# First loads in order of use, row norms from the transposed inputs, a last output block in three pieces, and attention outputs made with channels on partitions

## The chip, the core and the metric

The kernel runs on one core of a Trainium2 chip. TensorE (PE in the rows, with PEld its weight loads), VectorE (DVE), ScalarE (ACT), GpSimd (POOL) and SyncE (SP, which here only issues DMAs) each run their own instruction list in order; instructions on different engines wait for each other through semaphores. The metric is the device time of one execution in microseconds (us); less is better.

## The reference

One hybrid encoder layer over 256 tokens of width 2048, in float32. `h` is the normalised input, one large projection of it feeds three branches, and their outputs are gated, projected up, merged and projected once more:

```
h = rms_norm(x, norm_g);  proj = h @ w_in          # split into aq ak av az br bk bv bz bwd bad cq cz ga gb gc
aq, ak = rms_norm per head (8 heads x 128)
ya = chunked_band_attention(aq, ak, av, a_rel_bias) * silu(az)      # softmax over a band of keys, learned bias
yb = rwkv7_time_mix(br, bk, bv, bwd, bad, ...) * silu(bz)           # 16 heads x 64, a recurrence over the tokens
m  = rms_norm(mem, mem_norm_g);  mk, mv = split(m @ w_mem_kv)       # 256 memory tokens
yc = memory_cross_attention(rms_norm(cq), rms_norm(mk), mv) * silu(cz)    # 4 heads x 256
merged = sigmoid(ga)*(ya @ w_up_a) + sigmoid(gb)*(yb @ w_up_b) + sigmoid(gc)*(yc @ w_up_c)
out = x + merged @ w_o
```

## The kernel before

All weights come as one stream of 185 chunks of 1 MB (128 partitions x 2048 floats), issued on the SP queue in the order of use (`wload`, L172 for the first chunk in two halves, L175 for the others), into the tile `raw` with two buffers. `wchunk` turns each half of a chunk into two pieces that TensorE can take: ACT casts it to `whi` (L185), DVE subtracts to get the rest, `wlo` (L187); each has four buffers. The activations are split in the same way (`xh`/`xl` for x, `mh`/`ml` for the memory, `yh`/`yl` for a branch's output, all with channels on partitions).

A projection (`proj`) runs 12 matmuls of 512 columns for each half chunk, 4 each of `whi`·`xh` (L204), `whi`·`xl` (L205) and `wlo`·`xh` (L209). Here this is called a tick. `proj_cm` makes the same products with channels on partitions: 24 matmuls of 256 columns a tick (L222, L223, L225). After each tick, pieces of work that is written as generators (`spawn`, `tick`, `finish`) are put between the matmuls: norms, attention heads, the RWKV recurrence. A generator that yields n is left alone for n ticks. From this program a scheduler makes one fixed list for each engine.

The stages are, in order: the memory projection (32 ticks, ending in the product of `diag` and `ones` at L377); cq and cz, and cross-attention C; the RWKV inputs; gates and up-projections of C; attention A in two halves of four heads (`attn`), while RWKV quarters run between the ticks; gates and up-projections of A, then of B; the output projection in four blocks of 512 columns.

What the change touches:

- The head. `load_split` reads the transposed memory `memT` (then `xT`) in four pieces `xraw` of 512 KB, two buffers, and splits them (ACT L275, DVE L276). The sum of squares of each token is taken from a second copy of the same data with tokens on partitions: `row_rstd` loads `mem` and `x` as `tokraw` (8 DMAs of 512 KB, L259), and ACT squares and sums them (L260).
- `norm_T` normalises q and k, and transposes them; two transposes' worth of PSUM per yield.
- Cross-attention heads (`c_head`) and band-attention heads (`a_head`), one generator each: scores, softmax on DVE and ACT without the division, a transpose of the probabilities (L870), a copy to `apT` (L872), and the product with the values (L876 to L878), whose result has tokens on partitions. DVE divides by the denominator and multiplies by silu(z) there (L881), into `y`. Before the up-projection `to_T` transposes `y` in 16 pieces of 128x128 per branch (L325) and splits it (L326, L327).
- The last heads of A are forced to their end before the gate projection of A:

```
    for g in agen:
        finish(g)
    ...
    yt = spawn(to_T(y_a, yh, yl, 0, 8))
    for j in range(4):
        branch(yh, yl, j, False, yt)
```

- The end. After the last block's matmuls DVE adds the residual in two operations of 128x512 (L958), and SP and ACT each issue one DMA of 256 KB (L960).

Of the kernel before, what the change touches and what calls it, by code (L numbers as in the profile page):

```python
# [17 lines left out]
S = 256  # L18
P = 128
# [14 lines left out]
LATE = 3  # L34
NY = (0, 1, 4)
# [4 lines left out]
def weight_plan():  # L40
# [19 lines left out]
    def attn(h):  # L60
        for o in (O_AQ, O_AK, O_AV, O_AZ):
            plan.append(("in", o + h * 512, 16, 512))

# [30 lines left out]
def _build(ctx, nc, tc, A, out, dbg):  # L94
# [71 lines left out]
    def wload():  # L166
# [12 lines left out]
    def wchunk():  # L179
        raw = first.pop() if first else next(wload())  # L180
# [32 lines left out]

    def proj_cm(xh, xl):
# [24 lines left out]
    V.memset(warm, 0.0)  # L239
    SC.activation(warm[:, 0:1], warm[:, 0:1], AF.Square)  # L240
# [13 lines left out]
    def row_rstd(st_pool, src, dst):  # L254
        ss = t(sm, [P, 2, 2], "ss", bufs=2)
# [5 lines left out]
        G.tensor_tensor(out=dst, in0=ss[:, :, 0], in1=ss[:, :, 1], op=ALU.add)  # L261
        rsqrt_small(dst, dst, 2, 1.0 / D, EPS)

    def load_split(st_pool, src, goff, h, l, mid=None):
        for c in range(4):
            if c:
                yield 2
            raw = t(st_pool, [P, 4, S], "xraw", bufs=2)
            for hf in range(2):
                nc.sync.dma_start(raw[:, hf * 2:hf * 2 + 2, :], src[:, c * 4 + hf * 2:c * 4 + hf * 2 + 2, :])  # L270
                if mid is not None and c == 0 and hf == 0:
                    next(mid)
            for k in range(4):
                kt = c * 4 + k
                SC.activation(h[:, kt, :], raw[:, k, :], AF.Copy, scale=vec[:, goff + kt:goff + kt + 1])  # L275
                V.scalar_tensor_tensor(out=l[:, kt, :], in0=raw[:, k, :], scalar=vec[:, goff + kt:goff + kt + 1],  # L276
                                       in1=h[:, kt, :].bitcast(F32), op0=ALU.mult, op1=ALU.subtract)
# [745 lines left out]
```

## Time and profile before

| | |
|---|---|
| median of 3 runs | 1175.42 us (1173.82 to 1178.39) |
| the profiled execution's own time, its span | 1177.95 us, 1175.9 us |
| TensorE busy, granted clock over the span | 1155.9 us (98%), 0.996 |
| VectorE, ScalarE, GpSimd busy | 784.1, 528.3, 164.2 us |
| HBM read and written | 211.14 MB, 3.67 MB |

Times in the rows are us from the start of the span unless marked ns. A line of the timeline can stand for several equal instructions (x4); its duration is then that of all. What stands in brackets is the idle time of the engine just before, and what ended it.

### The profile page before, as it was taken

What the parts mean: (1) busy time and instruction counts of PE and PEld (TensorE: products, weight loads), DVE (VectorE), ACT (ScalarE), POOL (GpSimd) and SP (SyncE); (2) the same over time, 40 slices, a digit from 0 to 9 for tenths busy, and PEclk for the clock granted to TensorE, in tenths of its full rate; (3) what the DMA queues carried; (4) which work ended last, traced back from release to release, by engine and by line L of the source; (5) the groups of instructions that cost most, each with busy time, mean ns of one, the idle gap of its engine ahead of it and who ended that gap; (6) DMA issues with size and microseconds to landing.
All of it is one profiled execution on the core that took longest, in us unless ns stands there. A gap on an engine that the chain in (4) does not pass through costs nothing.

```text
span 1175.9 us, 15987 instructions
## 1 busy us (share of the span) xinstructions
PE 1155.9 (98%) x6186; PEld 938.6 (80%) x6186; DVE 784.1 (67%) x1320; ACT 528.3 (45%) x654; POOL 164.2 (14%) x234
## 2 busy tenths in 40 slices
PE   7999999999999999999999999999999999999998
PEld 6778888889779778878897778777778877888886
DVE  5574555547959656979685878846787855557443
ACT  6764444445633434444543535543443343444331
POOL 0100000033010214010214110203101203300000
PEclk9999999999999999999999999999999999999999
DMA  8856545465554644554643455454455564555662
GB/s 306 315 217 230 184 140 179 152 199 195 181 213 146 230 167 134 185 205 167 209 162 108 143 189 175 161 179 144 143 190 200 175 206 152 204 179 173 221 218 103
DMA packets 37620, 216.87 MB, mean 184 GB/s; under 512 B 5166, under 2 KB 6958, under 8 KB 13994
## 3 DMA queue, kind: packets, MB, share of 16 engines
q1 hardware_dynamic: 30528, 202.70, 49.5%
q0 software_dynamic: 3936, 9.44, 3.0%
q10 hardware_dynamic: 3082, 3.73, 1.0%
q8 instruction: 48, 0.79, 0.3%
q14 instruction: 26, 0.21, 0.1%
HBM read 211.14 MB, written 3.67 MB: 183 GB/s over the span
## 4 chain that ended last, share of the span: by engine, by line
PE 85%; DVE 5%; DMA 5%; ACT 2%; issue 2%; POOL 1%; SPq 0%; DVEq 0%; ACTq 0%; POOLq 0%
PE pp L204 23%; PE pp L209 23%; PE pp L205 23%; DMA raw<-in_wstream_dram 4%; PE pp L222 3%; PE pp L225 3%; PE pp L223 3%; DVE wlo L187 2%; ACT whi L185 1%; PE ps L325 1%; PE ps L600 1%; PE ps L420 1%; PE ps L396 1%; PE ps L724 1%; PE ps L731 1%
## 5 line engine op out<-in xcount | busy, mean ns | idle before, releaser
L187 DVE TENSOR_TENSOR wlo<-raw,whi 128x1024 fp32r<-128x1024 f32 x370 | 455.2, 1242 | 291.6 <-ACT whi L185 290.1
L185 ACT CAST whi<-raw 128x1024 fp32r<-128x1024 f32 x370 | 382.2, 1049 | 567.2 <-PE pp L205 315.5
L204 PE MATMUL pp<-whi,xh 128*128 128x512 f32 x896 | 363.9, 406 | 0.0
L205 PE MATMUL pp<-whi,xl 128*128 128x512 f32 x896 | 355.7, 397 | 0.0
L209 PE MATMUL pp<-wlo,xh 128*128 128x512 f32 x896 | 246.5, 397 | 3.8 <-DVE wlo L187 3.8
L209 PEld LDWEIGHTS pp<-wlo,xh 128*128 128x128 f32 x896 | 168.5, 188 | 45.7 <-DVE wlo L187 5.1
L204 PEld LDWEIGHTS pp<-whi,xh 128*128 128x128 f32 x896 | 168.7, 188 | 40.2 <-ACT whi L185 1.1
L205 PEld LDWEIGHTS pp<-whi,xl 128*128 128x128 f32 x896 | 168.9, 188 | 38.1 <-issue 0.5
L204 PE MATMUL pp<-whi,yh 128*128 128x512 f32 x192 | 77.3, 403 | 0.0
L205 PE MATMUL pp<-whi,yl 128*128 128x512 f32 x192 | 76.1, 396 | 0.0
L222 PE MATMUL pp<-xh,whi 128*128 128x256 f32 x272 | 67.4, 286 | 0.0
L223 PE MATMUL pp<-xl,whi 128*128 128x256 f32 x272 | 65.5, 279 | 0.0
L204 PE MATMUL pp<-whi,mh 128*128 128x512 f32 x128 | 52.5, 412 | 8.1 <-ACT mh L275 6.3
L209 PE MATMUL pp<-wlo,yh 128*128 128x512 f32 x192 | 52.6, 395 | 0.0
L222 PEld LDWEIGHTS pp<-xh,whi 128*128 128x128 f32 x272 | 51.0, 188 | 0.9 <-issue 0.6
L205 PE MATMUL pp<-whi,ml 128*128 128x512 f32 x128 | 51.5, 404 | 0.0
L223 PEld LDWEIGHTS pp<-xl,whi 128*128 128x128 f32 x272 | 51.1, 188 | 0.5 <-issue 0.2
L205 PE MATMUL pp<-whi,gl 128*128 128x512 f32 x128 | 50.9, 398 | 0.0
L204 PE MATMUL pp<-whi,gh 128*128 128x512 f32 x128 | 50.5, 394 | 0.0
L204 PEld LDWEIGHTS pp<-whi,yh 128*128 128x128 f32 x192 | 36.1, 188 | 8.7 <-issue 0.3
L209 PEld LDWEIGHTS pp<-wlo,yh 128*128 128x128 f32 x192 | 36.1, 188 | 8.7
L205 PEld LDWEIGHTS pp<-whi,yl 128*128 128x128 f32 x192 | 36.1, 188 | 8.1
(231 smaller groups left out, 1219.4 us busy)
## 6 DMA issues: line engine op xcount, KB each, us to landing
raw<-in_wstream_dram SPq DMA_DIRECT2D x184, 1024.0 KB, 4.9
xraw<-in_memT_dram SPq DMA_DIRECT2D x8, 256.0 KB, 7.2
tokraw<-in_mem_dram SPq DMA_DIRECT2D x4, 512.0 KB, 7.0
xraw<-in_xT_dram SPq DMA_DIRECT2D x8, 256.0 KB, 6.7
tokraw<-in_x_dram SPq DMA_DIRECT2D x4, 512.0 KB, 5.9
Tu<-scrt POOLq DMA_DIRECT2D x4, 512.0 KB, 5.5
xr<-in_x_dram POOLq DMA_DIRECT2D x8, 256.0 KB, 4.1
out_dram<-xr POOLq DMA_DIRECT2D x6, 256.0 KB, 3.3
```

Source lines behind the costliest of these rows:

```text
L185: SC.copy(hi, sl)
L187: V.tensor_tensor(out=lo, in0=sl, in1=hi.bitcast(F32), op=ALU.subtract)
L204: T.matmul(acc[tt], xh[:, kt + k2, sl], hv[:, k2], start=(kt + k2 == 0), stop=False)
L205: T.matmul(acc[tt], xl[:, kt + k2, sl], hv[:, k2], start=False, stop=False)
L209: T.matmul(acc[tt], xh[:, kt + k2, sl], lv[:, k2], start=False, stop=(last and k2 == 1))
L222: T.matmul(acc, hv[:, k2], xh[:, kt + k2, :], start=(kt + k2 == 0), stop=False)
L223: T.matmul(acc, hv[:, k2], xl[:, kt + k2, :], start=False, stop=False)
L225: T.matmul(acc, lv[:, k2], xh[:, kt + k2, :], start=False, stop=(kt + k2 == 15))
L325: T.transpose(bank[:, kk, tt * P:tt * P + P], src[:, tt, (k + kk) * P:(k + kk + 1) * P], ident)
L396: T.matmul(sc[:, tt, :], cqT[:, hh * 2 + k, tt * P:tt * P + P], mkT[:, hd * 2 + k, :], start=(k == 0), stop=(k == 1))
L420: T.matmul(pv[:, tt, :], pT[:, k, tt, :], mv[:, k, hd * 256:(hd + 1) * 256], start=(k == 0), stop=(k == 1))
L600: T.matmul(scs[par][:, c].rearrange("p a u -> p (a u)"), BK[rs, b, c].rearrange("p a u -> p (a u)"), AX[rs, b, c, par:par + 2, :].rearrang ...
```

## The change

- Head: the first chunk comes in three pieces (512, 512 and 1024 columns) and the first piece of `memT` in three, in turn; `vec` goes to the ACT queue; 16 small matmuls on a constant tile run on TensorE before the first weight lands (`WARMUP`). `mem` is no longer read and `x` only for the residual: each `xraw` piece is squared in place by ACT once it is split, DVE adds the four rows of it into `part` (`sq_part`), and TensorE sums over partitions with `ones` (`row_rstd`).
- cz and az are made by `silu_T` with channels on partitions, by `proj_cm` in 128-column blocks instead of `proj` in one of 512.
- Heads go in pairs (`c_heads`, `a_heads`). DVE scales the probabilities by 1/denominator before the transpose. The operands of the product with the values are swapped, so its result has channels on partitions: `split_y` multiplies by silu(z) and writes the split pair `yth`, `ytl` directly. `to_T` is gone for C and A.
- The gate projection of A's first block comes first, and then the heads are brought to their end (`branch`).
- `norm_T` and `to_T` issue eight transposes together instead of four.
- The last output block is made in three accumulators (`proj_last`): token tile 0, then token tile 1 in two halves of 256 columns, with the last two ticks' operands held, so that each part ends, is added and stored for itself.

```
+            for a, b in ((0, 512), (512, 1024), (1024, 2048)):
+                nc.sync.dma_start(raw[:, a:b], A["wstream"][i][:, a:b])
...
+    def sq_part(st_pool, raw, part, c):
+        SC.activation(raw, raw, AF.Square)
+        V.tensor_tensor(out=raw[:, 0:2, :], in0=raw[:, 0:2, :], in1=raw[:, 2:4, :], op=ALU.add)
...
+            V.tensor_tensor(out=raw[:, 0, :], in0=raw[:, 0, :], in1=raw[:, 1, :], op=ALU.add)
+            V.tensor_tensor(out=part, in0=part, in1=raw[:, 0, :], op=ALU.add)
+    def row_rstd(tot, dst):
+        bank = psum([P, 2])
         for tt in range(2):
-            for hf in range(2):
-                xt = t(st_pool, [P, 1024], "tokraw", bufs=2)
-                nc.sync.dma_start(xt, src[tt * P:(tt + 1) * P, hf * 1024:(hf + 1) * 1024])
-                SC.activation(xt, xt, AF.Square, accum_out=ss[:, tt, hf:hf + 1])
+            T.matmul(bank[:, tt:tt + 1], tot[:, tt * P:tt * P + P], ones[:, 0:1], start=True, stop=True)
+        V.tensor_copy(dst, bank)
...
+    def silu_T(pl, xh, xl, dst):
+        for i in range(4):
+            acc = proj_cm(xh, xl)
+            zr = t(pl, [P, 512], "qn", bufs=2)[:, :S]
+            V.tensor_tensor(out=zr, in0=acc, in1=rstd_bc, op=ALU.mult)
+            SC.activation(dst[:, i, :], zr, AF.Sigmoid)
+            V.tensor_tensor(out=dst[:, i, :], in0=zr, in1=dst[:, i, :], op=ALU.mult)
+    def split_y(pl, pv, z, yh, yl):
+        y = t(pl, [P, 512], "qn", bufs=2).rearrange("p (a b) -> p a b", b=S)
+        V.tensor_tensor(out=y, in0=pv, in1=z, op=ALU.mult)
+        SC.copy(yh, y)
+        V.tensor_tensor(out=yl, in0=y, in1=yh.bitcast(F32), op=ALU.subtract)
...
+    wld = wload()
+    raw0 = next(wld)
+    xr0 = t(mp, [P, 4, S], "xraw", bufs=2)
+    nc.scalar.dma_start(vec, A["vec"])
+    nc.sync.dma_start(xr0[:, 0:1, :], A["memT"][:, 0:1, :])
+    next(wld)
+    nc.sync.dma_start(xr0[:, 1:2, :], A["memT"][:, 1:2, :])
+    nc.sync.dma_start(xr0[:, 2:4, :], A["memT"][:, 2:4, :])
+    next(wld)
...
+    for i in range(WARMUP):
+        T.matmul(wps[:64, :64], warm, warm, start=True, stop=True)
...
-            finish(yt)
+        for g in yt or ():
+            finish(g)
...
+    def a_heads(half, h0, qT, kT, av, zT):
+        bias = a_bias(half * 4 + h0)
+        yield 1 + h0
+        scs = [psum([P, 384]) for _ in range(2)]
...
+        for i in range(2):
+            bt, sc = bias[:, i, :], scs[i]
+            pr = t(ap_, [P, 384], "apr", bufs=2)
...
+            V.reciprocal(den, den)
+            V.tensor_scalar(out=pr[:, 0:128], in0=pr[:, 0:128], scalar1=den[:, 0:1], scalar2=None, op0=ALU.mult)
+            V.tensor_scalar(out=pr[:, 128:384], in0=pr[:, 128:384], scalar1=den[:, 1:2], scalar2=None, op0=ALU.mult)
+            prs.append(pr)
+        yield 4
+        pts = [psum([P, 3, P]) for _ in range(2)]
+        pTs = []
+        for i in range(2):
+            for b in range(3):
+                T.transpose(pts[i][:, b, :], prs[i][:, b * P:(b + 1) * P], ident)
...
+        yield 2
+        pv = psum([P, 2, S])
+        for i in range(2):
+            hc = slice((h0 + i) * P, (h0 + i) * P + P)
+            T.matmul(pv[:, i, :], av[:, 0, hc], pTs[i][:, 0:2].rearrange("p a b -> p (a b)"), start=True, stop=False)
+            T.matmul(pv[:, i, P:S], av[:, 1, hc], pTs[i][:, 2], start=False, stop=True)
+        ks = slice(half * 4 + h0, half * 4 + h0 + 2)
+        split_y(ap_, pv, zT[:, h0:h0 + 2, :], yah[:, ks, :], yal[:, ks, :])
...
+        if j == 3:
+            for acc, tt, c0, n in proj_last(gh, gl, 16, 2):
+                V.tensor_tensor(out=xr[:, tt, c0:c0 + n], in0=acc, in1=xr[:, tt, c0:c0 + n], op=ALU.add)
+                eng = nc.scalar if c0 else nc.sync
+                eng.dma_start(out[tt * P:(tt + 1) * P, j * 512 + c0:j * 512 + c0 + n], xr[:, tt, c0:c0 + n])
```

The order of ACT at the program's start, before. `raw` is the weight chunk, `xraw` a piece of `memT`, `mh` its rounded split; the numbers tell buffers of one name apart.

```order
L185 CAST whi_122<-raw_105 128x1024
L275 ACTIVATE mh_103<-xraw_108,vec_72 128x256 x2
L185 CAST whi_126<-raw_105 128x1024
L275 ACTIVATE mh_103<-xraw_108,vec_72 128x256 x2
L275 ACTIVATE mh_103<-xraw_154,vec_72 128x256 x4
L351 DMA cst_73<-in_cst_dram 128x384
L352 DMA eye_3_74<-in_eye_dram 128x256
L185 CAST whi_167<-raw_165 128x1024
L185 CAST whi_171<-raw_165 128x1024
```

The same place on ACT now.

```order
L442 CAST whi_138<-raw_105 128x512
L308 ACTIVATE mh_103<-xraw_107,vec_72 128x256
L442 CAST whi_138<-raw_105 128x512
L308 ACTIVATE mh_103<-xraw_107,vec_72 128x256 x3
L291 ACTIVATE xraw_107<-xraw_107 128x1024
L451 CAST whi_140<-raw_105 128x1024
L308 ACTIVATE mh_103<-xraw_183,vec_72 128x256 x4
L428 DMA cst_73<-in_cst_dram 128x384
L429 DMA eye_3_74<-in_eye_dram 128x256
L291 ACTIVATE xraw_183<-xraw_183 128x1024
L191 CAST whi_200<-raw_198 128x1024
L191 CAST whi_204<-raw_198 128x1024
```

A square of 128x1024 (L291) now stands ahead of the cast of the first chunk's second half, and another ahead of the cast of the second chunk (`raw_198`).

DVE in the second half of attention A, before: `apr` are the probabilities of one head, `Xu` and `tmu` belong to the RWKV loop. The rows begin where the loop ends.

```order
L638 TENSOR_TENSOR Xu_6091<-Xu_6091,tmu_6139 128x8
L688 COPY BK_6615<-vL_1551 64x128
L642 COPY tmx_6375<-Xu_6091 128x256
L688 COPY BK_6615<-vL_1551 64x128 x7
L688 COPY Tu_6614<-vL_1551 64x128 x8
L187 TENSOR_TENSOR wlo_6549<-raw_6541,whi_6547 128x1024
L854 SCALAR_TENSOR_TENSOR apr_6419<-ps_6416,bias_6344 128x128
L856 SCALAR_TENSOR_TENSOR apr_6419<-ps_6416,bias_6344 128x256
L859 TENSOR_REDUCE nmx_6422<-apr_6419 128x1
L860 TENSOR_REDUCE nmx_6422<-apr_6419 128x1
```

The same place on DVE now.

```order
L743 TENSOR_TENSOR Xu_6470<-Xu_6470,tmu_6559 128x8
L793 COPY Tu_7034<-vL_1824 64x128
L747 COPY tmx_6852<-Xu_6470 128x256
L793 COPY Tu_7034<-vL_1824 64x128
L793 COPY BK_7035<-vL_1824 64x128 x2
L193 TENSOR_TENSOR wlo_6970<-raw_6966,whi_6968 128x1024
L956 SCALAR_TENSOR_TENSOR apr_6778<-ps_6772,bias_6654 128x128
L958 SCALAR_TENSOR_TENSOR apr_6778<-ps_6772,bias_6654 128x256
L961 TENSOR_REDUCE nmx_6781<-apr_6778 128x1
L962 TENSOR_REDUCE nmx_6781<-apr_6778 128x1
```

Softmax of heads 2 and 3 stands at the same place on DVE as before, behind the whole loop.

TensorE there, before: `pp` are projection accumulators (those of zb), `apT` transposed probabilities, `avv` the values, and the last row transposes the probabilities of head 2.

```order
L209 MATMUL pp_6222<-wlo_6450,xh_89 128x512 x2
L876 MATMUL ps_6480<-avv_6023,apT_6402 128x128
L877 MATMUL ps_6480<-avv_6023,apT_6402 128x128
L878 MATMUL ps_6480<-avv_6023,apT_6402 128x128
L204 MATMUL pp_6221<-whi_6452,xh_89 128x512
...
L209 MATMUL pp_6222<-wlo_6454,xh_89 128x512 x2
L870 MATMUL ps_6502<-cst_73,apr_6419 128x128 x3
```

TensorE there now.

```order
L215 MATMUL pp_6659<-wlo_6897,xh_88 128x512 x2
L985 MATMUL ps_6927<-apT_6877,avv_6361 128x256
L986 MATMUL ps_6927<-apT_6877,avv_6361 128x128
L985 MATMUL ps_6927<-apT_6879,avv_6361 128x256
L986 MATMUL ps_6927<-apT_6879,avv_6361 128x128
L976 MATMUL ps_6936<-cst_73,apr_6778 128x128 x3
L976 MATMUL ps_6937<-cst_73,apr_6791 128x128 x3
L210 MATMUL pp_6658<-whi_6899,xh_88 128x512
```

The transposes of heads 2 and 3 now stand together, one tick earlier than that of head 2 stood: ahead of the last tick of zb's projection instead of behind it.

## Rows read from the trace of the kernel before

**Rows 1.** The page, busy time of each engine and share of the span.

```profile
PE 1155.9 (98%) x6186; PEld 938.6 (80%) x6186; DVE 784.1 (67%) x1320; ACT 528.3 (45%) x654; POOL 164.2 (14%) x234
```

**Rows 2.** What TensorE waited for: us in total, times, longest.

```profile
PE pp L209 <- DVE wlo L187: 4.3, 4, 2.5
PE ps L876 <- ACT apT L872: 2.2, 1, 2.2
PE pp L204 <- ACT whi L185: 1.8, 2, 1.5
PE ps L870 <- ACT apr L863: 0.5, 1, 0.5
```

**Rows 3.** Timeline of the head: start, duration, engine, line, operation, tiles, count [idle].

```profile
4.52 1.04 ACT L185 CAST whi<-raw 128x1024 fp32r<-128x1024 f32 x1 [2.30 <-DMA raw<-in_wstream_dram]
6.34 1.22 PE L204 MATMUL pp<-whi,mh 128*128 128x512 f32 x2 [6.34 <-ACT mh L275]
8.48 1.04 ACT L185 CAST whi<-raw 128x1024 fp32r<-128x1024 f32 x1 [1.80 <-DMA raw<-in_wstream_dram]
9.66 1.71 ACT L275 ACTIVATE mh<-xraw,vec 128x256 fp32r<-128x256 f32 x4
10.70 2.46 DVE L276 SCALAR_TENSOR_TENSOR ml<-xraw,vec,mh 128x256 fp32r<-128x256 f32 x6
13.47 2.00 ACT L185 CAST whi<-raw 128x1024 fp32r<-128x1024 f32 x2 [1.30 <-DMA raw<-in_wstream_dram]
14.93 0.40 PE L204 MATMUL pp<-whi,mh 128*128 128x512 f32 x1
...
39.80 0.50 PE L204 MATMUL pp<-whi,mh 128*128 128x512 f32 x1 [1.54 <-ACT whi L185]
72.06 1.20 PE L209 MATMUL pp<-wlo,mh 128*128 128x512 f32 x4 [0.50 <-DVE wlo L187]
104.02 0.59 PE L377 MATMUL ps<-diag,ones 128*128 128x256 f32 x2
```

**Rows 4.** TensorE with 128-column transposes (L325), and with `proj_cm` (L225).

```profile
1047.13 0.60 PE L325 MATMUL ps<-cst,merged 128*128 128x128 f32 x4
...
1047.80 0.39 PE L205 MATMUL pp<-whi,yl 128*128 128x512 f32 x1
...
207.20 1.10 PE L225 MATMUL pp<-xh,wlo 128*128 128x256 f32 x8
```

**Rows 5.** Timeline of the second half of attention A.

```profile
708.22 0.19 DVE L636 TENSOR_TENSOR tmu<-Tu,Xu 128x31 f32<-128x31 f32 x1 [2.64 <-DMA Tu<-scrt]
744.08 1.10 PE L209 MATMUL pp<-wlo,xh 128*128 128x512 f32 x4
744.12 1.77 DVE L688 COPY Tu<-vL 64x128 f32<-64x128 f32 x8
745.01 0.39 PE L876 MATMUL ps<-avv,apT 128*128 128x128 f32 x2
745.93 1.23 DVE L187 TENSOR_TENSOR wlo<-raw,whi 128x1024 fp32r<-128x1024 f32 x1
747.07 0.28 DVE L854 SCALAR_TENSOR_TENSOR apr<-ps,bias 128x128 f32<-128x128 f32 x1
747.60 0.28 DVE L859 TENSOR_REDUCE nmx<-apr 128x1 f32<-128x128 f32 x1
749.64 0.17 DVE L866 RECIPROCAL rden<-den 128x2 f32<-128x2 f32 x1
```

**Rows 6.** Windows: us, busy PE, PEld, DVE, ACT, POOL, granted clock, DMA share, GB/s.

```profile
676.00:680.00 4.00, 1.55 (x4) 1.13 (x4) 3.77 (x5) 1.99 (x2) 0.17 (x1) 0.78 0.00 0
756.00:760.00 4.00, 4.00 (x21) 3.72 (x21) 2.35 (x5) 0.74 (x2) 0.00 (x0) 0.59 0.49 201
```

**Rows 7.** Timeline of the end.

```profile
1170.78 1.29 DVE L958 TENSOR_TENSOR xr<-pp,xr 128x512 f32<-128x512 f32 x2 [9.36 <-PE pp L209]
1172.10 0.36 ACTq L960 DMA_DIRECT2D out_dram<-xr  x1
```

More of the change, by code (lines that the diff above doesn't have):

```diff
@@ L60, in attn @@
     def attn(h):
-        for o in (O_AQ, O_AK, O_AV, O_AZ):
+        for o in (O_AQ, O_AK, O_AV):
             plan.append(("in", o + h * 512, 16, 512))
+        for i in range(4):
+            plan.append(("in", O_AZ + h * 512 + i * 128, 16, 128))
     rk(0)
@@ L212, in proj, with proj_last, run @@
         return acc
+    def proj_last(xh, xl, nk, split):
+        accA = pp.tile([P, 512], F32, name=nm("pp"), tag="pp", bufs=4)
+        accB = [pp.tile([P, 512], F32, name=nm("pp"), tag="pp", bufs=4) for _ in range(2)]
+        parts = [(accA, 0, 0, 512)] + [(accB[i][:, :256], 1, i * 256, 256) for i in range(2)]
+        kt = 0
+        def run(part, kt, hv, lv):
+            acc, tt, c0, n = part
+            sl = slice(tt * P, tt * P + P)
+            cs = slice(c0, c0 + n)
+            for k2 in range(2):
+                T.matmul(acc, xh[:, kt + k2, sl], hv[:, k2, cs], start=(kt + k2 == 0), stop=False)
+                T.matmul(acc, xl[:, kt + k2, sl], hv[:, k2, cs], start=False, stop=False)
+            for k2 in range(2):
+                T.matmul(acc, xh[:, kt + k2, sl], lv[:, k2, cs], start=False, stop=(kt + k2 == nk - 1))
+        held = []
+        while kt < nk:
+            for hi, lo in wchunk():
+                held.append((kt, hi.rearrange("p (k n) -> p k n", n=512), lo.rearrange("p (k n) -> p k n", n=512)))
+                kt += 2
+                if kt <= nk - 2 * split:
+                    for part in parts:
+                        run(part, *held[-1])
+                    held.clear()
+                tick()
+        for part in parts:
+            for h in held:
+                run(part, *h)
+            yield part
     def proj_cm(xh, xl):
@@ L270, in load_split @@
                 nc.sync.dma_start(raw[:, hf * 2:hf * 2 + 2, :], src[:, c * 4 + hf * 2:c * 4 + hf * 2 + 2, :])
-                if mid is not None and c == 0 and hf == 0:
-                    next(mid)
             for k in range(4):
[L274 to L277, printed above, removed]
+                split_kt(raw[:, k, :], goff, c * 4 + k, h, l)
+            sq_part(st_pool, raw, part, c)
     def norm_T(pl, acc, rstd, nh, hd, gcols, dst):
@@ L468, in _build @@
         finish(g)
-    dump("y_c", y_c)
     c_st.close()
@@ L884, in _build @@
     agen = []
     def attn(half):
-        cols = slice(half * 512, half * 512 + 512)
         acc = proj(xh, xl, 16)
@@ L898, in attn @@
         evac_scale(acc, rstd_x, av)
-        acc = proj(xh, xl, 16)
-        evac_silu(acc, y_a[:, :, cols])
+        zT = t(ap_, [P, 4, S], "azT")
+        silu_T(ap_, xh, xl, zT)
         finish(kn)
-        bias = [a_bias(half * 4)]
-        for h in range(4):
-            agen.append(spawn(a_head(half, h, qT, kT, av, bias), 2 * h))
+        for h0 in (0, 2):
+            agen.append(spawn(a_heads(half, h0, qT, kT, av, zT)))
     rk_proj(2)
@@ L911, in _build @@
     evac_silu(proj(xh, xl, 16), zb0)
-    for g in agen:
-        finish(g)
+    for j in range(4):
+        branch(yah, yal, j, False, agen if j == 0 else None)
     at_st.close()
-    dump("y_a", y_a)
-    g_st = ExitStack()
-    gp = pool(g_st, "ga")
-    yh = t(gp, [P, 8, S], "yh", F32R)
-    yl = t(gp, [P, 8, S], "yl", F32R)
-    yt = spawn(to_T(y_a, yh, yl, 0, 8))
-    for j in range(4):
-        branch(yh, yl, j, False, yt)
-    g_st.close()
     dump("merged_a", merged)
```

268 lines of the change are left out of this document (142 added, 126 removed).

## The prediction

> **What bounds the kernel now.** I read the busy times first, then TensorE's list of waits, then the timeline around each wait, and the granted clock of the windows behind them. TensorE is busy for 98% of the span, DVE for 67% [rows 1]. So only what TensorE executes, what it waits for, and the two ends of the program count; work taken from or given to DVE or ACT costs something only where TensorE then waits for it. TensorE has four places of loss [rows 2, 3]: the start, where its first matmul comes at 6.34; the memory stage (1.54 at 39.80, 0.50 at 72.06, the rest of the 1.8 on `whi` in the same stage); 3.8 of the 4.3 on `wlo`, which fall between 656 and 681 in an RWKV quarter; and the last heads of attention A, 2.2 on `apT` and 0.5 on `apr`. After two of these the clock drops to its lower level, 1.2 GHz, for a time: the window from 676 shows 0.78 and that from 756 shows 0.59 [rows 6]. The matmuls of one tick take 12 x 0.233 = 2.80 us: the four that begin at 744.08 give way at 745.01 [rows 5].
>
> The sum is made against the profiled execution's own 1177.95 us (span 1175.9 and 2.05 around it). That is 2.5 above the median of the runs; I carry the difference over to the median.
>
> **The head.** The start is earlier, but the start is not what decides. The second half of the first chunk is there at 8.48 and the second chunk at 13.47: each cast ends a wait for its DMA [rows 3]. The bytes ahead of the second chunk in the queues are the same as before, since the eight `tokraw` loads stand behind it. So the landing stays near 13.4, and what can be won early is lost again in the wait for it. Now a square stands ahead of each of these casts on ACT, and it works in place: it has to wait until DVE has read the piece for `ml`. By hand: the last two `mh` of the first piece end at about 7.9, their `ml` at 8.3; the square (I price it as the cast of the same 1024 columns, 1.04) ends at 9.3, the cast of the third part of chunk 0 at 10.35; four `mh` take 1.71 [rows 3] and end at 12.05. On DVE that half's `wlo` (1.14, from 745.93 to 747.07 [rows 5]) ends at 11.5 and four `ml` at 0.41 (six took 2.46 [rows 3]) at 13.1; the second square ends at 14.1 and the first cast of chunk 1 at 15.2. The third tick, which began at 14.93, begins at about 15.2: later, in spite of a first matmul at about 5.0.
>
> From there I find no wait of TensorE: chunk 2 is issued near 11.6, no longer kept behind `tokraw` loads, and each later cast by hand is done 2 to 5 us before its tick. The 30 ticks left take 84.0 and the 16 transposes of the two key norms 1.75, which puts the product at L377 at 101.0 instead of 104.02 [rows 3]: a gain of 3.0. What goes is the late issue of chunks 2 and 4, the 1.54 and the 0.50. Ends: if the second chunk were no limit, 5.0 + 32 x 2.80 + 1.75 = 96.4, a gain of 7.6; if the new way to the norm (DVE copy, GpSimd, ACT) holds ACT for another 1.5, as the old one did before 39.80, and the third tick comes 1 later, a gain of 0.5. I take 2.8, near the hand schedule.
>
> The 16 small matmuls ahead of the first weight bear on the clock. Before, the four matmuls of the first two rows of TensorE in the head stood 0.43 to 0.61 apart, half the rate of later ones (the two from 6.34 take 1.22 [rows 3]). The Trainium skill, TensorE: Matmul & The Clock Gate, "What's actually happening", holds that the throttled state is the default and that activity releases it. By that the second tick would run at 2.4 GHz and end at 13.2; with the clock as the head showed it before, it would end at 15.5. The third tick's cast at 15.2 lies between, so the gain is 3.0 by the one and 2.7 by the other.
>
> **Transposes.** 32 transposes of `y` for C and A go. Four cost 0.67 - 0.23 = 0.44, from 1047.13 to the second matmul behind them at 1047.80 [rows 4]; 32 are 3.5 us of TensorE time in a stage where it never idles. Gain 3.5. Their casts and subtractions move into `split_y`, one 512-wide operation each, beside other matmuls.
>
> **silu by `proj_cm`.** 384 matmuls of 512 columns become 768 of 256. Eight of 256 take 1.10 [rows 4] and four of 512 take 1.10 [rows 5]; the rows differ by less than their last digit, which over 96 such groups is at most 1.0. I take 0.5 lost, the ends 0 and 1.0. The last block's smaller matmuls add 0.1 in the same way, the 4 matmuls with `ones` as much again at most.
>
> **End.** Before, DVE added the first of the last two accumulators from 1170.78, when it was done, and both until 1172.07; the last DMA was issued at 1172.10, 3.8 before the end [rows 7]. The last accumulator now ends where the second one did, two matmuls behind the first, at about 1171.25 for DVE, and only 256 columns are added then, some 0.4 (half of 0.65, and a start): 1171.65, 0.4 earlier. The DMA is half as large; if all its time went with size that would be 1.9, if none, nothing; I take 0.2, near the lower end. Gain 0.6, ends 0.4 and 2.3.
>
> **Last heads of A.** The wait of 2.2 + 0.5 and the slow window behind it (4 x 0.41 = 1.6) go, 4.3 in all, because the heads are no longer forced through behind each other. But I see a new wait on the same softmax. DVE works without a break from 708.22, where the RWKV loop starts, to 745.93 [rows 5], and softmax of head 2 stands behind that loop in both orders. Between these points the new order lacks 12 copies of 64x128 (8 take 1.77, so 2.65), two 512-wide products (1.3), two of 128 (0.6) and one `wlo` (1.14), and has four scalings (a 128 and a 256 wide one 0.53, from 747.07 to 747.60 [rows 5]: 1.06) and seven operations of 256 (0.33 each, 2.3) more. Head 2's softmax begins 2.3 earlier, at 744.7. The chain to its reciprocal took 2.57 (747.07 to 749.64 [rows 5]); one `wlo`, a copy and the scaling lie in it now, so the probabilities are ready at 749.0, and those of head 3, behind five more copies, at 750.9. TensorE, however, wants them one tick earlier than before: the tick that ended at 745.01, then both heads' value products (0.65 more than the one head's there), 0.2 for `proj_cm`: 745.9. It waits 3.1 for head 2 and 1.6 for head 3, 4.7, and behind that loses some 1.3 to the lower clock (between the 0.9 and 1.6 of [rows 6]). 6.0 against 4.3: 1.7 lost. Ends: 4.3 gained if DVE comes to head 2 five us sooner, 4 lost if it comes two later.
>
> **Hidden edits.** DVE gets 0.7 x 8 and 0.33 x 14 more for the sums of squares, and the products, scalings and splits of the pairs; with 33% of DVE idle [rows 1] I cost them at nothing outside the place above. Uncovered, a pair's softmax takes 6.2 from its first operation to the second head's end (744.7 to 750.9; 2.3 of it are one `wlo` and RWKV's copies), while C's pairs leave two ticks, 5.6, and A's four. C may wait 0 to 1.5, the first half of A as much; I take nothing. The 3.8 on `wlo` from 656 on stay: the same DVE burst stands there. Grouped transposes of the norms change nothing in sum.
>
> Sum: -2.8 - 3.5 + 0.5 + 0.2 - 0.6 + 1.7 = -4.5. 1177.95 becomes 1173.45, the median 1170.9.
>
> **Rivals.**
> - Heads 2 and 3 do not wait. The loop on DVE starts with a DMA [rows 5]; if that lands some 5 us sooner against TensorE's ticks, the 4.3 go and nothing comes: the sum is then -4.5 - 1.7 - 4.3 = -10.5, the median 1164.9. Against it: the rows of DVE ahead of the loop are as good as the same.
> - The head reaches its floor of 96.4: 7.6 for 2.8, median 1166.1. For it: 4 MB less are read in the first 60 us. Against it: the second chunk's landing, and ACT's squares ahead of the casts.
> - The head gives nothing (0.5 for 2.8): median 1173.2. For it: ACT works in order, and each square can hold a cast back.
> - Slower: pairs wait on DVE wherever they stand. The place is the pair's transposes, at C twice and in A four times; the price is the pair's 6.2 plus the `wlo` that the order puts between, less the ticks left. It decides from the point where DVE starts a pair more than half a tick late at C (5.6 left) or 5 late at A. Then C costs 2 x 3 with the lower clock, the first half of A 6.0, the second 2 more: +14, median 1184.9. For it: the second half, where I count on it already. Against it: C and A's first half have no RWKV loop of that length on DVE.
>
> **Numbers.** The forecast case 0.45 (its own range 1167.5 to 1174), no wait of heads 2 and 3 0.20, head at its floor 0.10, head without gain 0.13, slower 0.12. The bound between a change and none is 0.5%, 5.9 us: faster is below 1169.5, slower above 1181.3. Faster: both early cases and a third of the forecast's, 0.45; slower 0.11, nearly all of its case; the rest, 0.44, within. The range goes from 1162, where part of the first two rivals together lies, to 1179, part of the slow case.
>
> **What would show it.** First matmul near 5 but the third tick at 15 to 15.5; squares on ACT ahead of the casts at about 8.3 and 13.1; L377's successor at 101; no wait of TensorE between 16 and 100; no `to_T` of `y_c`, `y_a`; waits of about 3 and 1.6 on the transposes of `apr` in the second half of A, with a lower clock behind, and none in the first; 3.8 on `wlo` in the RWKV quarter before. It is wrong if the memory stage ends before 98 or after 103, if the last heads wait under 2 or over 8, or if C waits over 2.

## The result, and the profile after

The changed kernel takes 1162.82 us (median of 4 runs, 1162.67 to 1164.07), the kernel before 1176.62 beside it: 0.9887 of the time, with an interval of 0.9864 to 0.991. That is 13.8 us less against a forecast of 4.5. The profiled execution is of 1162.67 us, its span 1160.9, the granted clock 0.998.

The page of the changed kernel, busy time of each engine, share and instructions (it answers to [rows 1]):

```profile
PE 1141.2 (98%) x6610; PEld 961.0 (83%) x6610; DVE 804.7 (69%) x1378; ACT 528.9 (46%) x655; POOL 167.5 (14%) x232
```

TensorE is busy for 14.7 us less, and yet it executes 424 instructions more. The 32 transposes that went are worth 3.5 of it; no other step of the forecast takes work from it. So something made each matmul shorter. The list of what TensorE waited for in the changed kernel (us in total, times, longest; one row of 0.2 is left out; it answers to [rows 2]) shows at the same time that waits took no part in the gain; they add up to 16.1, against 15.3 before (of which 6.3 ahead of the first matmul):

```profile
PE pp L215 <- DVE wlo L193: 3.9, 3, 2.8
PE pp L210 <- ACT whi L191: 3.5, 2, 2.0
PE ps L423 <- ACT warm L420: 2.7, 1, 2.7
PE ps L976 <- ACT BKt L758: 2.1, 1, 2.1
PE ps L976 <- DVE apr L968: 1.3, 1, 1.3
PE pp L210 <- ACT mh L308: 0.9, 1, 0.9
PE pp L210 <- ACT whi L451: 0.9, 1, 0.9
PE ps L705 <- DVE AX L717: 0.6, 1, 0.6
```

Where the time went is seen in TensorE's timeline, at the group of four 512-column matmuls that [rows 5] show from 744.08 to 745.01. First such a group on `xh` in the changed kernel, with the instruction behind it, then one on `yth`, then eight of 256 columns in `proj_cm`:

```profile
742.41 1.07 PE L215 MATMUL pp<-wlo,xh 128*128 128x512 f32 x4
743.31 0.59 PE L985 MATMUL ps<-apT,avv 128*128 128x256 f32 x2
...
889.68 1.10 PE L215 MATMUL pp<-wlo,yth 128*128 128x512 f32 x4
890.62 0.40 PE L210 MATMUL pp<-whi,yth 128*128 128x512 f32 x1
...
260.49 1.12 PE L262 MATMUL pp<-xh,wlo 128*128 128x256 f32 x8
261.45 0.28 PE L259 MATMUL pp<-xh,whi 128*128 128x256 f32 x1
```

In the kernel before, the instruction behind the eight of [rows 4]:

```profile
208.14 0.81 PE L396 MATMUL ps<-mkT,cqT 128*128 128x256 f32 x3
```

Four on `xh` now give way after 0.90 us (before: 0.93), four on `yth` after 0.94, and eight of 256 columns after 0.96 (before 0.94, from 207.20 to 208.14). Averaged over all matmuls that directly follow another of the same size without a wait, from start to start, 512 columns take 227.6 ns (before 233.3), 512 columns on `yth` and `ytl` 233.3, 256 columns 119.9 (before 117.6). The clock is at its upper level in both (granted 0.996 before and 0.998 now over the span). Nothing in these instructions was changed; what differs is where their operands lie in a partition of the on-chip memory. In the built programs the weights `whi`, `wlo` start at 160 modulo 256 both times. `xh`, `xl`, `mh`, `yh`, `gh` start at 224 before and at 160 after, because small tiles that the change no longer needs lay in front of them (the pool of small tiles shrank from 832 to 512 bytes, and a reserved area from 16384 to 4096). `yth` starts at 224.

### The profile page after: what moved, and what is told of

The parts are those of the page before. It is cut to its first block, busy times and chain, and to the rows that moved or that the text cites. A ratio compares the mean times of both kernels' runs of the same rounds, so it can differ in the third digit from the quotient of the medians.

```text
span 1160.9 us, 16874 instructions
## 1 busy us (share of the span) xinstructions
PE 1141.2 (98%) x6610; PEld 961.0 (83%) x6610; DVE 804.7 (69%) x1378; ACT 528.9 (46%) x655; POOL 167.5 (14%) x232
## 4 chain that ended last, share of the span: by engine, by line
PE 82%; DVE 9%; DMA 4%; issue 2%; ACT 1%; POOL 1%; SPq 0%; ACTq 0%; POOLq 0%; DVEq 0%
PE pp L210 21%; PE pp L211 20%; PE pp L215 20%; PE pp L259 4%; PE pp L260 4%; PE pp L262 4%; DVE wlo L193 3%; DMA raw<-in_wstream_dram 3%; DVE Xu L743 1%; DVE tmu L741 1%; DMA Tu<-scrt 1%; PE pp L232 1%; PE pp L234 1%; PE pp L231 1%; ACT whi L191 1%
## 5 line engine op out<-in xcount | busy, mean ns | idle before, releaser
L210 PE MATMUL pp<-whi,xh 128*128 128x512 f32 x768 | 309.2, 403 | 1.5 <-ACT whi L191 1.5
L211 PE MATMUL pp<-whi,xl 128*128 128x512 f32 x768 | 300.8, 392 | 0.0
L259 PE MATMUL pp<-xh,whi 128*128 128x256 f32 x528 | 131.3, 287 | 0.0
L260 PE MATMUL pp<-xl,whi 128*128 128x256 f32 x528 | 129.6, 284 | 0.0
L259 PEld LDWEIGHTS pp<-xh,whi 128*128 128x128 f32 x528 | 101.2, 192 | 1.1 <-issue 0.6
L260 PEld LDWEIGHTS pp<-xl,whi 128*128 128x128 f32 x528 | 101.4, 192 | 0.6 <-issue 0.2
L262 PE MATMUL pp<-xh,wlo 128*128 128x256 f32 x528 | 74.1, 283 | 0.0
L262 PEld LDWEIGHTS pp<-xh,wlo 128*128 128x128 f32 x528 | 68.1, 192 | 0.0
L210 PE MATMUL pp<-whi,yth 128*128 128x512 f32 x128 | 51.9, 405 | 0.0
L211 PE MATMUL pp<-whi,ytl 128*128 128x512 f32 x128 | 50.5, 395 | 0.0
```

Of the source, the lines that this page charges most:

```text
L210: T.matmul(acc[tt], xh[:, kt + k2, sl], hv[:, k2], start=(kt + k2 == 0), stop=False)
L211: T.matmul(acc[tt], xl[:, kt + k2, sl], hv[:, k2], start=False, stop=False)
L259: T.matmul(acc, hv[:, k2], xh[:, kt + k2, :], start=(kt + k2 == 0), stop=False)
L260: T.matmul(acc, hv[:, k2], xl[:, kt + k2, :], start=False, stop=False)
L262: T.matmul(acc, lv[:, k2], xh[:, kt + k2, :], start=False, stop=(kt + k2 == 15))
```

## The experiments

The theory after this was that the distance of the two start addresses modulo 256 sets the spacing. The experiments move tiles without changing a matmul. In the first pair the edit is one line ahead of `mhalf`, the same in both kernels:

```
+    G.memset(t(sm, [P, 16], "pad"), 0.0)      # 64 unused bytes
```

**e1: before, 64 bytes more.** 

> The kernel before with one unused tile of 64 bytes per partition in the pool of small tiles, so that every tile behind it (xh, xl, mh, ml, yh, yl, gh, gl) starts 64 bytes further; the list of instructions is otherwise the same. Theory A (the start address of the operand that TensorE loads as weights sets the spacing of the matmuls: xh stood at 96 modulo 128 bytes before and stands at 32 in the changed kernel): the 512-column matmuls go from 233.3 ns apart to about 227, the 256-column ones of proj_cm from 117.7 to 119.9; 4032 x 6.4 ns less and 816 x 2.1 ns more, -24 us, about 1152 to 1157 (some of it may come back as waits). If the period is 256 bytes and not 128, no change or an unknown one. Theory B (the spacing follows from the work beside the matmuls, which the change altered): 233.3 ns and 1176 us as before.

Measured: 1175.55 us, ratio 0.9995 (0.9981 to 1.0009). `xh` stands at 32, 128 from the weights; 512 columns take 232.7 ns, 256 columns 119.3. No change: a distance of 128 is not as good as 0.

**e2: after, 64 bytes more.** 

> The changed kernel with the same unused tile of 64 bytes: xh, mh, yh, gh start at 96 modulo 128 again. Theory A: the matmuls on them go back to 233.3 ns (512 columns) and 117.7 (256 columns): about 3300 x 6.3 ns more and 1680 x 2.1 ns less, +15 to +17 us, 1178 us, a little slower than the kernel before; the rest of the change is then worth nothing or less. Theory B: 227 ns and 1163 us as they are.

Measured: 1173.37 us, ratio 0.9969 (0.9956 to 0.9982). `xh` is back at 224, the distance of before, and so are the spacings: 233.3 and 117.5 ns. TensorE's timeline of e2, the same four matmuls and their successor:

```profile
746.33 1.09 PE L215 MATMUL pp<-wlo,xh 128*128 128x512 f32 x4
747.26 0.59 PE L986 MATMUL ps<-apT,avv 128*128 128x256 f32 x2
```

0.93 again. So 64 unused bytes take back some 10 us (10.6 between the two medians, 9.6 by their ratios to the kernel before). At equal addresses the change itself is worth 3.5 against the kernel before beside it (1176.9; by the interval 2.1 to 5.2), and 4.3 between the two profiled executions (spans 1175.9 and 1171.6), of which that of before (1177.95) was above its median.

**e3: before, the reserved area cut to 4096 bytes.**

```
-    nc = bacc.Bacc("TRN2", target_bir_lowering=False, num_devices=1)
+    nc = bacc.Bacc("TRN2", target_bir_lowering=False, num_devices=1, dynamic_dma_scratch_size=4096)
```

> The kernel before with the reserved area at the start of the on-chip memory at 4 KB instead of 16 KB, as the changed kernel has it; all tiles shift by 12288 bytes, a multiple of 256. Theory A: no change, 233.3 ns and 1176 us. Rival C (the smaller reserved area is what made the matmuls faster, through GpSimd's DMAs or the absolute addresses): 227 ns and 1155 to 1163 us.

Measured: 1176.33 us, ratio 0.999 (0.9979 to 1.0001), spacings 233.3 and 117.7. It shifts `xh` and the weights by 12288, a multiple of 256, and does nothing.

**e4: a kernel of matmuls alone.** It leaves the layer out and copies x to the output. Eight stationary and eight moving tiles start 32 bytes apart modulo 256 (`sa` 128, `sb` 160, ... `sh` 96; `ma` to `mh` the same), and each pair runs 24 times, with 512 columns (L40, stationary `s`) and with 256 (L45, stationary `m`). 

> Not the layer: x is copied to the output, and beside it TensorE runs 64 groups of 24 matmuls of 512 columns (weights from tile sa to sh, moving columns from tile ma to mh) and then 64 groups of 24 of 256 columns with the two roles exchanged. The tiles' starts step by 32 bytes: sa and ma at 128 modulo 256, sb and mb at 160, and so on to sh and mh at 96. No other engine works. Theory A: within the 512-column groups the spacing depends on the weight tile alone, 227 ns for starts of 32 modulo 128 and 233 for 96, the same for all m at a given s, and in the second half of the grid 117.7 to 120 by tile. Theory B: all 512-column groups have one spacing.

Groups of e4 by line and tile (moving, then stationary tile; count; busy us, mean ns of one). The mean is longer than the spacing, since a matmul overlaps the next one:

```profile
L40 PE MATMUL pa<-mb,sb 128*128 128x512 f32 x24 | 5.6, 391 | 0.0
L40 PE MATMUL pa<-mb,sh 128*128 128x512 f32 x24 | 5.7, 392 | 0.0
L40 PE MATMUL pa<-mb,sd 128*128 128x512 f32 x24 | 5.8, 396 | 0.0
...
L45 PE MATMUL pa<-sb,mb 128*128 128x256 f32 x24 | 3.0, 283 | 0.0
L45 PE MATMUL pa<-sh,mb 128*128 128x256 f32 x24 | 2.9, 277 | 0.0
L45 PE MATMUL pa<-sd,mb 128*128 128x256 f32 x24 | 3.0, 279 | 0.0
```

With 512 columns the pairs at distance 0 (here `mb`, `sb`) are the shortest, 227 to 228 ns from start to start (only `ma`, `sa`, which comes first, has longer matmuls at its beginning); the eight whose stationary tile lies 64 below the moving one (`sh`) follow with 229; the other 48 take 232 to 234, `sd`, the distance of before, among them. The expectation's theory A, in which the stationary tile alone decides, is out: with `sb` the spacing is 228 or 233 by the moving tile. With 256 columns distance 0 is slow (119.3 to 119.7), and a moving tile 64 below the stationary one is fast, but only for five of the eight such pairs (113.7 to 114.7; the other three 117.7 to 117.8). That part isn't settled by the distance alone.

**e5: before, 192 bytes more**, the line of e1 with 48 floats, so that `xh` starts at 160.

```
+    G.memset(t(sm, [P, 48], "pad"), 0.0)      # 192 unused bytes
```

> The kernel before with an unused tile of 192 bytes in the pool of small tiles: xh, mh, yh, gh then start at 160 modulo 256, as whi and wlo do. Theory A2 (what counts is the distance modulo 256 between the start of the weight operand and that of the moving operand; the grid gives 226.7 ns for 0, 229.3 for -64 and 233 to 234 for the others): 512-column matmuls from 233.3 to 226.7, 256-column ones from 117.7 to 119.9; 4032 x 6.6 less and 816 x 2.2 more, -25 us, 1151 to 1157 after some new waits. That is more than the whole change gave. Theory B2 (64 bytes more slowed the changed kernel for another reason): 233 ns and 1176 us.

Measured: 1159.82 us, ratio 0.9857 (0.9841 to 0.9873), span 1158.9; 512 columns take 227.7 ns, 256 columns 119.9. TensorE's timeline of e5:

```profile
733.72 1.08 PE L209 MATMUL pp<-wlo,xh 128*128 128x512 f32 x4
734.63 0.38 PE L877 MATMUL ps<-avv,apT 128*128 128x128 f32 x2
```

192 unused bytes in the old kernel give as much as the whole change (by the medians 3 us more, but the two intervals overlap). The expectation was 25 us; the gain is 16. The shorter matmuls are there: 4032 x 5.6 ns less and 816 x 2.3 ns more make 20.7 us less, not 25, since 512 columns came to 227.7 and not to the 226.7 of the grid. More waits came with them: 6.3 on `wlo` (before 4.3) and 2.3 on `whi` (1.8 [rows 2]), 2.5 more in sum. What took the last 2 us stays open.

**e10: after, 192 bytes more.** `xh` at 96, 64 below the weights; the edit is e5's line.

> The changed kernel with 192 bytes more in the pool of small tiles: xh, mh, yh, gh at 96 modulo 256, 64 below whi and wlo. By the grid 512-column matmuls take 229.3 instead of 226.7 there (some 3200 x 2.5 = 8 us more) and 256-column ones 114 to 117 instead of 119.9 (1680 x 3 to 6 = 5 to 10 us less): 1161 to 1166 us, with both spacings as named. If the period or the sign were wrong, 233 ns or 119.9 would show.

Measured: 1164.59 us, ratio 0.9905 (0.9885 to 0.9924). Spacings 229.5, 233.3 on `yth`, and 114.0 with 256 columns. TensorE's timeline of e10, twice eight of 256 columns on the same tiles:

```profile
201.08 1.11 PE L262 MATMUL pp<-xh,wlo 128*128 128x256 f32 x8
202.02 3.62 PE L494 MATMUL ps<-mkT,cqT 128*128 128x256 f32 x16
...
261.08 1.07 PE L262 MATMUL pp<-xh,wlo 128*128 128x256 f32 x8
261.99 0.28 PE L259 MATMUL pp<-xh,whi 128*128 128x256 f32 x1
```

0.91 at 261.08 against 0.96 in the changed kernel. All three spacings came as the grid had them. But the 114.0 is a mean of two levels: those from 201.08 give way after 0.94, on the same tiles at the same distance modulo 512 and with the clock at its upper level (granted 1.00 from 200 to 204 and from 260 to 264). At this distance the 256-column matmuls run at some 113 or some 118 ns for several ticks and then change; so the distance alone doesn't decide it.

**e6: after, every pair aligned.** `yth` moves to 160, and `proj_cm` writes its weights 64 bytes further on, for its moving operand to lie 64 below them.

```
-    def wchunk():
+    def wchunk(o=0):
...
-            hi = t(wp, [P, 1024], "whi", F32R, bufs=4)
+            hi = t(wp, [P, 1088], "whi", F32R, bufs=4)[:, o:o + 1024]
...
-        for hi, lo in wchunk():
+        for hi, lo in wchunk(16):
...
+    G.memset(t(ycp, [P, 16], "padr"), 0.0)
...
```

The tiles of `wlo` are cut in the same way, and the reserved area goes from 4096 to 2048 bytes to make room.

> The changed kernel with starts chosen from the grid: yth and ytl at 160 modulo 256 (an unused tile of 64 bytes beside them), and for proj_cm the weight pieces written 64 bytes further into tiles that are 256 bytes longer (the reserved area goes from 4096 to 2048 bytes to make room). Theory A2: the up-projections of C and A go from 233.3 to 226.7 ns (384 x 6.6 = 2.5 us) and the 256-column matmuls from 119.9 to 114 (1680 x 5.9 = 9.9 us): 1150.5 us, 1149 to 1156. Rival (with ACT, DVE and DMAs beside it the gain of the grid does not come for 256 columns): 119 to 120 ns, 1160 us.

Measured: 1159.52 us, ratio 0.9857 (0.9834 to 0.9881). Spacings 227.6, 227.3 on `yth`, and 117.2 with 256 columns instead of 114. It is e10's pair of levels again, with the slow one in most groups: eight from 129.81 give way after 0.94, eight from 458.29 after 0.91. New waits took part of the rest, 4.7 on `whi` (3.5 in the changed kernel) and 2.1 on `AX` (0.6).

**e11: e6 at e10's place**, moving operands at 96 and `proj_cm`'s weights at 160; beside e6's edit:

```
+    G.memset(t(cp, [P, 48], "padc"), 0.0)
...
-    G.memset(t(ycp, [P, 16], "padr"), 0.0)
+    G.memset(t(ycp, [P, 32], "padr"), 0.0)
```

> The kernel after with all rows of xh and yth and the weights of RWKV's first projections at a start address of 96 (mod 256), so that the 512-column matmuls read both operands at distance 0, and the weights of the 256-column matmuls (proj_cm) 64 bytes behind their moving operand, at 160 against 96, which is the place where e10 measured 114.0 ns (e6 stood at another place with the same distance and measured 117.2). Theory (distance and place set the spacing): 512 columns 227 to 228 ns, 256 columns 114 ns; against e6 that is 1680 x 3.2 ns = 5.4 us less matmul time, 1154 to 1157 us. Rival 1 (the place matters in another way): the 256-column matmuls stay at 117 ns and the time is e6's, 1159 to 1160. Rival 2 (faster matmuls only wait for weight chunks): spacing 114 ns, but waits on whi grow by as much as the matmuls shrink, 1159 to 1160 as well, told apart from rival 1 by the spacing.

Measured: 1159.02 us, ratio 0.985 (0.9834 to 0.9867). 512 columns take 227.6 ns, but 256 columns 117.1, and not e10's 114; most groups run at the slow level. Rival 1: the start addresses modulo 256 don't fix the 256-column matmul. e6 and e11 are clearly faster than the kernel before. By their medians they are also 3 to 4 us faster than the changed kernel, but their intervals overlap with its own, with each other and with that of e5.

**e7: after, with the squares written two pieces later** and three `xraw` buffers.

```
...
-            sq_part(st_pool, raw, part, c)
+            pend.append((raw, c))
+            while len(pend) > 2 or c == 3 and pend:
+                sq_part(st_pool, pend[0][0], part, pend.pop(0)[1])
...
```

> The changed kernel with each square and its three additions issued two pieces of memT (or xT) later, and a third buffer for these pieces; nothing is left out. Theory H (the squares, which wait for DVE and stand ahead of the casts on ACT, moved the third tick from 14.9 to 17.0): the third tick starts with the landing of the second chunk plus a cast, about 14.6, and the 2.4 us stay: 1160.4 us. Rival (the landing itself comes later, or the later pieces of memT become late instead): third tick after 16.4, or a new wait before 60; 1162 to 1163 us.

Measured: 1164.44 us, ratio 0.989 (0.9862 to 0.9918). TensorE's third tick in e7:

```profile
15.87 0.50 PE L210 MATMUL pp<-whi,mh 128*128 128x512 f32 x1 [2.00 <-ACT whi L191]
```

The scheduler put squares ahead of the casts again (the second stands on ACT at 13.83, the cast behind it), so this run doesn't test what it was made for.

**e9: after, with the squares of two of the four pieces of `memT` left out** (the memory's norms are then taken from half its channels).

```
-            sq_part(st_pool, raw, part, c)
+            if c >= 2 * c0:
+                sq_part(st_pool, raw, part, c - 2 * c0)
...
-        sq_part(mp, xr0, partm, 0)
```

> The changed kernel without the squares and additions of the first two pieces of memT (the memory's norm is then taken from the other two); in the run before, where they were only written later, the scheduler had put them ahead of the casts again. Theory H (these two squares hold the casts of chunk 0's second half and of chunk 1): the second tick starts about 1 us sooner, the third with the landing of chunk 1 plus a cast, at 14.5 to 15.0 instead of 17.0, and the end of the memory stage comes 2 us sooner, at 99.8. Rival (the chunk's landing): third tick after 16.4.

Measured: 1163.99 us, ratio 0.989 (0.9855 to 0.9925), from two runs of 1160.77 and 1167.21. TensorE's two waits of e9 in the memory stage, the cast that ends the second, the issue of its chunk on SP, and DVE's subtraction ahead of that:

```profile
14.92 0.50 PE L210 MATMUL pp<-whi,mh 128*128 128x512 f32 x1 [1.34 <-ACT whi L191]
...
33.85 0.50 PE L210 MATMUL pp<-whi,mh 128*128 128x512 f32 x1 [2.03 <-ACT whi L191]
...
32.75 2.00 ACT L191 CAST whi<-raw 128x1024 fp32r<-128x1024 f32 x2 [3.75 <-DMA raw<-in_wstream_dram]
...
24.07 1.00 SPq L179 DMA_DIRECT2D raw<-in_wstream_dram  x1
...
22.82 1.22 DVE L193 TENSOR_TENSOR wlo<-raw,whi 128x1024 fp32r<-128x1024 f32 x1
```

Without the squares the third tick comes at 14.92 instead of 17.00: they were what held it. But the two us don't last. At 33.85 TensorE waits 2.03 for a chunk that landed at 32.75 (the cast's wait ends with the landing); it was issued only at 24.07, when DVE had ended the subtraction (at 24.04) that still read its buffer. Behind this wait the clock falls to its lower level for a time (granted 0.88 from 32 to 36 and 0.70 from 36 to 40). The stage ends at 103.64, no sooner than the 101.77 of the changed kernel.

**e8: after, heads two ticks later**, ahead of the transposes:

```
-        yield 4
+        yield 6
```

> The changed kernel with the transposes of a pair of A's heads six ticks behind its scores instead of four. Theory D (TensorE asks for the probabilities of the second half while DVE is still in the RWKV loop): the waits of 2.1 and 1.3 on the transposes go, -3.4 us, 1159.4. Rival (the two buffers of apr let the softmax of heads 2 and 3 start only when heads 0 and 1 are transposed, so the wait moves to heads 2 and 3): waits of 3 to 5 us there, 1162 to 1166 us.

Measured: 1162.02 us, ratio 0.9876 (0.9861 to 0.9891). TensorE's wait on the transposes in e8:

```profile
PE ps L976 <- DVE apr L968: 2.5, 1, 2.5
```

One wait of 2.5 in place of 2.1 and 1.3, and no time won that can be measured: the wait moves, and behind it the clock falls to its lower level for a time (granted 0.60 from 748 to 752), which it doesn't in the changed kernel.

## Why the prediction was right and wrong

The direction was right, the size was not: the step that failed stands in the first part of it, "The matmuls of one tick take 12 x 0.233 = 2.80 us". The prediction carried this over to the changed kernel, in the head (30 ticks at 2.80) and wherever it changes nothing. The sum has no term for where the operands lie. After, a tick of 512 columns takes 2.73. The measured median still lies at the lower edge of the stated range of 1162 to 1179; that is luck, since this edge was set for the first two rivals together, and what brought the kernel there is the spacing. Against e2, the same program at the old distance, 3216 matmuls of 512 columns are 5.7 ns shorter, 18.3 us, and 1680 of 256 columns 2.4 longer, 4.0: 14.3 less. Waits take 3.2 of that back (16.1 in the changed kernel against 12.9 in e2, whole lists), one of them at 394.05, here with ACT's cast:

```profile
394.05 0.51 PE L210 MATMUL pp<-whi,xh 128*128 128x512 f32 x1 [1.48 <-ACT whi L191]
...
392.95 1.99 ACT L191 CAST whi<-raw 128x1024 fp32r<-128x1024 f32 x2 [8.66 <-DMA raw<-in_wstream_dram]
```

A faster TensorE reaches the next chunk before it has landed. e2, on its side, loses at least 1.4 more in the head, where its clock falls (0.36 x 4 in the window from 16, below). That leaves 12.5 where the spans differ by 10.7; what makes up the last 2 us stays open.

Without that term the sum was near: -4.5 predicted, -3.5 (median) and -4.3 (span) measured with e2. That is luck too, for errors of opposite sign cancel. From before's profiled execution to that of e2 the head and the memory stage became 1.1 longer (104.02 to 105.14), where -2.8 was written. The second half of A with the RWKV work in it, from one product of `tmpA` to the next, became 2.9 shorter (650.97 to 842.55 before, 651.23 to 839.87 in e2), where its transposes, silu and heads had +0.2 in all. From there to the end it is 1.6 less, where -0.4 was written. Part by part:

**Head: mis-sized.** ACT's timeline in the head of the changed kernel, TensorE's third tick and the end of the stage (they answer to [rows 3]):

```profile
7.39 0.62 ACT L442 CAST whi<-raw 128x512 fp32r<-128x512 f32 x1 [1.94 <-DMA raw<-in_wstream_dram]
9.95 1.06 ACT L291 ACTIVATE xraw<-xraw 128x1024 f32<-128x1024 f32 x1 [0.67 <-DVE ml L309]
14.95 1.06 ACT L291 ACTIVATE xraw<-xraw 128x1024 f32<-128x1024 f32 x1 [1.39 <-DVE ml L309]
15.91 1.99 ACT L191 CAST whi<-raw 128x1024 fp32r<-128x1024 f32 x2
...
17.00 0.50 PE L210 MATMUL pp<-whi,mh 128*128 128x512 f32 x1 [1.99 <-ACT whi L191]
...
101.77 0.59 PE L474 MATMUL ps<-diag,ones 128*128 128x256 f32 x2
```

The mechanism is the one described: each square waits for DVE's `ml` and holds the cast behind it. But the hand schedule began too early. The chunk's second piece landed only at 7.39, so the first square stands at 9.95 and not at 8.3, the second at 14.95 and not at 13.1, and the third tick at 17.00 and not at 15.2. The end at 101.77 looks like the 101.0 of the prediction, but faster matmuls make some 2.2 of it (32 ticks of 12 x 5.7 ns); in e2 the stage ends at 105.14, 1.1 later than before instead of 2.8 earlier. Part of that is the clock behind the long wait, which the prediction left out of the head. Windows of e2 and of the changed kernel (us, busy PE, granted clock, DMA share, GB/s):

```profile
16.00:20.00 4.00, 3.14 (x8) 0.64 0.79 305
```

```profile
16.00:20.00 4.00, 3.00 (x13) 1.00 0.79 280
```

In e2 it falls to its lower level for a time, as in the profiles of e6, e10 and e11; in the changed kernel's own it doesn't. The head of before varies too: e1's ends its stage at 102.20, before's own at 104.02. So the head's gain is 0 at best, and any figure for it is uncertain by about 2 us. Nor did the program start earlier: the first matmul comes at 6.33, as before (6.34), and not near 5.0.

The 16 small matmuls on the constant tile did what was asked of them in this execution. TensorE's first rows in the changed kernel:

```profile
2.72 3.67 PE L423 MATMUL ps<-warm 128*64 128x64 f32 x32 [2.72 <-ACT warm L420]
6.33 0.50 PE L210 MATMUL pp<-whi,mh 128*128 128x512 f32 x1
6.66 0.39 PE L211 MATMUL pp<-whi,ml 128*128 128x512 f32 x1
```

The first two on weights are 0.33 apart and the next ones 0.23, where before the first ones stood 0.43 to 0.61 apart. This agrees with the sentence that the prediction took from the Trainium skill, TensorE: Matmul & The Clock Gate, "What's actually happening": activity releases the clock. In e9 the first two are still 0.60 apart, with the same small matmuls ahead. They also stand in the way: TensorE is at them until the first matmul begins, though `mh` was there from 5.45 on (ACT, 4.94 and 0.51 long), and the prediction had no term for that. By these rows neither decides, since the third tick waits for its cast either way; no run leaves the small matmuls out.

**Transposes and silu: near.** From the end of the memory stage to the first product of `tmpA`, with the 16 transposes of C in between, e2 takes 1.3 us less than before (105.14 to 301.22 against 104.02 to 301.41), near the 1.76 of the transposes less 0.25 for half of silu. That 256 columns cost as much as half of 512 holds in e2 (117.5 to 233.3); at distance 0 it doesn't (119.9 to 227.6), and the 768 that replace 384 of 512 columns cost 4.7 us there. The matmuls on `yth` lose another 2.2 (384 x 5.7 ns). The two would put e5 below the changed kernel, as the medians have it by 3 us, but within their intervals; no run shows that by itself.

**Attention: the wait was there, at another place.** TensorE, ACT and DVE in the second half of A of the changed kernel (it answers to [rows 5]):

```profile
737.98 0.93 PE L976 MATMUL ps<-cst,apr 128*128 128x128 f32 x6 [2.09 <-ACT BKt L758]
744.62 0.49 PE L976 MATMUL ps<-cst,apr 128*128 128x128 f32 x3
746.40 0.70 PE L976 MATMUL ps<-cst,apr 128*128 128x128 f32 x3 [1.29 <-DVE apr L968]
...
736.50 1.04 ACT L191 CAST whi<-raw 128x1024 fp32r<-128x1024 f32 x1 [4.70 <-DMA raw<-in_wstream_dram]
737.45 0.85 ACT L758 COPY BKt<-ps 128x384 f32<-128x384 f32 x2
...
703.89 0.19 DVE L741 TENSOR_TENSOR tmu<-Tu,Xu 128x31 f32<-128x31 f32 x1 [1.63 <-DMA Tu<-scrt]
739.75 0.28 DVE L956 SCALAR_TENSOR_TENSOR apr<-ps,bias 128x128 f32<-128x128 f32 x1
```

Head 2 doesn't wait at all. DVE begins its softmax at 739.75, 4.9 ahead of the transposes that want it, where the prediction had 1.2 (744.7 against 745.9); that is the end of its range where "DVE comes to head 2 five us sooner". Most of it is the start of DVE's loop, at 703.89 instead of 708.22: 4.3 sooner, 2.7 of it against TensorE's tick (742.41 and 744.08). From there to the softmax DVE takes 35.9 instead of 38.9, 3.0 less, near the 2.3 that the prediction counted. It left out the first and named it only as a rival. Head 3 waits 1.29 against 1.6. The other wait, 2.09, is that of heads 0 and 1, and not for softmax: their transposes write a `ps` bank, and by its named releaser that comes free with RWKV's copy L758. On ACT this copy stands behind a cast that waited until 736.50 for its chunk. The clock stays at 1.00 behind both (windows 736 to 740 and 744 to 748). So the step is some -0.9 by the trace (waits of 3.4 against the 4.3 of before) where +1.7 was written; e2, with waits of 1.9 and 1.1 and no fall of the clock there, has -1.3. The "no wait" rival was half right.

**End: between the ends.** DVE's last addition and the last issue of the changed kernel (they answer to [rows 7]):

```profile
1157.52 0.42 DVE L1053 TENSOR_TENSOR xr<-pp,xr 128x256 f32<-128x256 f32 x1 [1.01 <-PE pp L234]
1157.98 0.36 ACTq L1055 DMA_DIRECT2D out_dram<-xr  x1
```

2.9 us pass from the issue to the end, 3.8 before: a DMA of half the size gave 0.9 instead of 0.2. The whole step is -1.3 instead of -0.6.

The 3.8 on `wlo` in the RWKV quarter stayed (3.9), as predicted. The rival by which pairs wait on DVE everywhere fell: the list names no wait in C or the first half of A.

## What to carry to other kernels

Where a kernel is 98% matmul, look at the time from one matmul to the next before and after a change, and at the start addresses of the operands: any edit that adds or drops a tile can shift them, and here 64 or 192 unused bytes were worth more than everything that was rewritten. To judge a change by itself, bring both kernels to the same addresses first. And work taken from the path ends where the next chunk's landing or the next buffer is late: in e6, e8 and e9 the waits took back part or all of what was won.

## What was not expected of the hardware

With operands of four bytes a column, a matmul of 512 columns took 227 to 228 ns after another when its stationary and moving tile started at the same address modulo 256, 229 to 230 with the stationary one 64 below, and 232 to 234 at the other six distances of e4. The kernels of the layer, which stand at four of the eight distances (0, 64 below, 64 above, 128), agree. With 256 columns equal addresses were slow (119.3 to 119.9 ns). With the moving tile 64 below, the matmuls ran at one of two levels, some 113 and 118 ns, and one kernel showed both on the same tiles (e10 at 261.08 and 201.08); most groups ran at the fast one in e10 and at the slow one in e6 and e11. What decides that, and why the distance counts, is open: no view shows the memory's own accesses.
